# Down's last block: stores of the last results on one queue, one result turned right behind its product, and a product that goes on in another's banks

## The chip, the cores and the metric

One Trainium2 chip, one of its cores. The metric is the device time of one execution in microseconds, as a median of several runs.

## The reference

A decoder block on 512 tokens with 2048 channels, all in float32: three token mixers, an output projection, and a SwiGLU feed-forward network. Only its last line matters here:

```python
h2 = _rms_norm(x, norm2_g[l])
x = x + (jax.nn.silu(h2 @ w_gate[l]) * (h2 @ w_up[l])) @ w_down[l]
```

`w_down` is 5632 by 2048. The output is the residual plus this product.

## The kernel before, in words

Float32 matrix products are made of pieces. Every operand is split into a high part and a remainder, and each tile product is three matmuls (high by high, high by low, low by high; lines 1438 to 1440 in `Down.multiply`). The weights are split just ahead of their use by `split_up_to`: ScalarE copies the high part twice (into PSUM, line 268, and into SBUF, line 269), and VectorE subtracts it to give the low part `wl` (line 270). The weights of one piece of a product are a *unit*.

The two large products of the feed-forward network are computed by a seven-product scheme on 2 by 2 blocks. The products are numbered and run in `ORDER = (7, 1, 4, 6, 5, 2, 3)`. `Down` runs twelve blocks (`t`), which alternate between two groups of 512 columns (`g`) and go through six ranges of the inner dimension. The last block, number 11, has `end` set; blocks 10 and 11 have `final` set.

In one block each of the seven products is computed into two PSUM banks (`a` = 0 and 1). There are four such banks, used in turn, so that a product comes to stand in the banks of the one two before it. Products 7, 1, 5 and 2 start their banks afresh; 4, 6 and 3 go on in what 7, 1 and 5 left there (`fresh` in `product`). The last product of the last block (`tail`) is an exception: it starts all its banks afresh. When a product is complete, `done` puts the banks on the sums: `y[g, i, k, a]`, 128 by 512 tiles in SBUF. Sum (i, k) is channel half i and token half k. The banks go, after product 7, into sum (1,1); after 1 into (0,0); 4 into (1,0); 6 into (1,1), (0,1) and (1,0); 5 into (1,1) and, in the last block alone, into (0,1); 2 into (0,0); 3 into (0,1). Most of this is done by VectorE, which reads the bank (line 1448).

A complete sum must leave the chip with channels as rows. `turn_back` transposes it in 32 by 32 pieces on VectorE into a tile `z` (line 1355; it waits for the buffer of `z`). `put` stores one `z` with four DMAs of 128 KB, each in runs of 256 bytes (line 1365). Each DMA signals one of eight completion semaphores, which are dealt out in turn in the order of the program, whichever queue a DMA is issued on. A DMA waits on its queue until the DMA that had its semaphore before has landed.

Nothing schedules by itself: `later(n, ...)` puts a step in `evacs` or `extras`, and `run` takes the next entry of each list ahead of and behind each unit. `evacs` holds sums and turns, `extras` holds stores.

The last block ends like this. After product 6, sum (1,0) is turned and stored on SP's queue. After product 5, both `less` and both `add` run, then (1,1) is turned in two later steps, and its four stores are issued on **ACT's** queue. After product 2, ScalarE copies each of the two banks into SBUF (line 1486) and GpSimd adds the copies to sum (0,0) (line 1448 on POOL). Product 3 is the `tail` (lines 1393 to 1426). It runs in three pieces: n=0 is bank a=0 with 512 columns, n=1 bank a=1 with columns 0 to 255, n=2 bank a=1 with columns 256 to 511, which stands in the first bank of product 2. Behind the matmuls of n=0 VectorE gets the two turns of (0,0), whose `put` goes on SP, and then the sum of n=0 with (0,1) (line 1417) and half a turn; behind n=1 again a sum and half a turn, and a `put` of half size (four DMAs of 64 KB). Ahead of n=2, TensorE transposes the other half of a=0 into the bank pair `sides` (`turn(0)`, line 1403), which needs the sum of n=0. After the sum of n=2 it does the same for a=1 (`turn(1)`); VectorE and ScalarE copy `sides` into the two `end` tiles (line 1406), and two DMAs of 128 KB on SP's queue store them (line 1425). These are the last stores.

Of the kernel before, what the change touches and what calls it, by code (L numbers as in the profile page):

```python
# [17 lines left out]
T = 512  # L18
# [48 lines left out]
TH = T // 2  # L67
# [48 lines left out]
def kernel(ctx: ExitStack, tc: tile.TileContext, xT, wi, wo, wgu, wd, cst_in, outT):  # L116
    nc = tc.nc
# [19 lines left out]
    def slot(name, dt=F32, cols=T):  # L137
        return sp.tile([P, cols], dt, name=name, tag="s")

    def bank(name, cols=T, pool="banks"):  # L140
        return psum[pool].tile([P, cols], F32, name=name, tag="b")


    units = [wi[0][:, :TH], wi[0][:, TH:T], wi[0][:, T:], wi[1][:, :T], wi[1][:, T:]] + [wi[u] for u in range(2, 2 * N_IN)]
# [143 lines left out]
    def sums_now():  # L288
        for fn in sums.pop(at["use"], ()):
            fn()  # L290
# [38 lines left out]
    b = bank("idle")  # L329
    for i in range(WARM):  # L330
        nc.tensor.matmul(b, idle, idle[:, None, :].to_broadcast([P, NT, P]), start=True, stop=True)
    b = idle = None
# [101 lines left out]
    for k in range(KT):  # L434
# [21 lines left out]
        hi, lo = h_hl.pop(k)  # L456
# [22 lines left out]
    def project(name):  # L479
        b = bank(name, pool="tiles")  # L480
        for half in range(2):
            wh, wl = next_unit()
            for kk in range(8):
                k = 8 * half + kk
                s = slice(kk * P, (kk + 1) * P)
                mm3(b, wh[:, s], wl[:, s], h_hi[k], h_lo[k], k == 0, k == KT - 1)
                if kk == 3:
                    lows_now()
                if kk % 2 == 1:
                    ticks.tick()  # L490
        return b
# [445 lines left out]
    for name in PROJ[HEAD4:]:  # L937
# [4 lines left out]
        b = project(name)  # L942
# [17 lines left out]
    b = box = boxes = shared = None  # L960
# [81 lines left out]
    for half in range(2):  # L1042
        for i, n in enumerate(OUT_ORDER[half]):
            if half == 1 and i == 2:
                open_banks(banks=2, high=2)
            b = bank(f"o{half}_{n}", pool="tiles")
# [21 lines left out]
    b = m_hi = m_lo = r1b = mult_a = bias_a = bias_c = over = upper = None  # L1068
# [17 lines left out]
    evacs, extras = [], []  # L1086
# [10 lines left out]
    def run(queue):  # L1097

        for fn, *args in queue.pop(0) if queue else ():
            fn(*args)  # L1100

    def later(n, fn, *args, queue=evacs):
        while len(queue) <= n:
            queue.append([])
        queue[n].append((fn, *args))
# [59 lines left out]
    class Up:  # L1165
# [4 lines left out]
        def product(self, q):  # L1170
            banks = outs[:2]
            outs[:] = outs[2:] + banks
            for c in range(2):
                sums_now()
                run(evacs)
                wh, wl = next_unit()
                for a, b in enumerate(banks):
                    high, low = slice(a * P, (a + 1) * P), slice(TH + a * P, TH + (a + 1) * P)
                    for f in range(2):
                        x, s = ops[q, self.first + 2 * c + f], slice(f * T, (f + 1) * T)  # L1180
                        nc.tensor.matmul(b, x[:, high], wh[:, s], start=c == f == 0 and q in (7, 1, 5, 2), stop=False,  # L1181
                                         skip_group_check=True)
                        nc.tensor.matmul(b, x[:, high], wl[:, s], start=False, stop=False, skip_group_check=True)  # L1183
                        nc.tensor.matmul(b, x[:, low], wh[:, s], start=False, stop=c == f == 1, skip_group_check=True)  # L1184
                yield
                run(extras)
            later(0, self.done, self.first == 0, q, banks)
# [89 lines left out]
    y = {}  # L1277
# [70 lines left out]
    def turn_back(key, lo=0, hi=T):  # L1348

        g, i, k, a = key  # L1350
        if (g, i, k) not in pairs_out:
            name, c = BACK[g, i, k]
            pairs_out[g, i, k] = wp.tile([P, 1024], F32, name=f"z{g}{i}{k}", tag=f"raw{final_bufs[c][name]}", bufs=1)
        z = pairs_out[g, i, k].rearrange("p (b a j) -> p a b j", a=2, j=32)[:, a, lo // 32:hi // 32]
        nc.vector.transpose(z, y[key][:, lo:hi].rearrange("p (b j) -> p b j", j=32))
        if hi == T:
            y.pop(key)
# [10 lines left out]
    class Down:  # L1368
# [9 lines left out]
        def product(self, k, q):  # L1378
            banks = outs[:2]
            outs[:] = outs[2:] + banks  # L1380
            fresh = q in (7, 1, 5, 2)
            tail = self.end and k == 6
            units = []
            for c in range(2):
                sums_now()
                run(evacs)
                units.append((next_unit(), list(enumerate(self.pairs[2 * c:2 * c + 2]))))
                if not tail:
                    for a in range(2):
                        self.multiply(q, banks[a], units[c:], a, 0, T, c == 0 and fresh, c == 1)  # L1390
                    load_next(1, FEED)
                    run(extras)
            if tail:

                out = banks + outs[:1]
                sides = psum["high"].tile([P, 2, T], F32, name="sides", tag="h")
                last = [slot(f"end{c}")[:, :TH].rearrange("p (b a j) -> p b a j", a=2, j=32) for c in range(2)]

                def turn(a):

                    src = y[self.sum(0, 1, a)]
                    for c in range(2):
                        nc.tensor.transpose(sides[:, c, a * P:(a + 1) * P], src[:, TH + c * P:TH + (c + 1) * P], ident)
                    for c in range(2):
                        eng, copy = ((nc.vector, nc.vector.tensor_copy), (nc.scalar, nc.scalar.copy))[c if a else 1]
                        copy(last[c][:, :, a], sides[:, c, a * P:(a + 1) * P].rearrange("p (b j) -> p b j", j=32))

                for n, (a, lo, hi) in enumerate(((0, 0, T), (1, 0, TH), (1, TH, T))):
                    if n == 2:
                        turn(0)  # L1410
                    self.multiply(q, out[n], units, a, lo, hi, True, True)
                    if n == 0:
                        for b in range(2):
                            turn_back(self.sum(0, 0, b))
                        put(self.g, 0, 0)
                    t = y[self.sum(0, 1, a)][:, lo:hi]
                    nc.vector.tensor_add(t, t, out[n][:, lo:hi])
                    if n < 2:
                        turn_back(self.sum(0, 1, a), 0, TH)
                    if n == 1:  # L1420
                        put(self.g, 0, 1, 0, TH)
                turn(1)
                for c in range(2):
                    to = 512 * self.g + TH + c * P
                    nc.sync.dma_start(outT.rearrange("n p t -> (n p) t")[to:to + P, TH:], last[c].rearrange("p b a j -> p (b a j)"))
                return
            if self.drops:
                for j in self.pairs:
                    acts.pop((q, j))
            later(0, self.done, q, banks)  # L1430
# [35 lines left out]
        def done(self, q, banks):  # L1466
            for a, b in enumerate(banks):
                if q == 7:
                    self.add(1, 1, a, b)
                elif q == 1:  # L1470
                    self.add(0, 0, a, b)
                elif q == 4:
                    self.add(1, 0, a, b)
                elif q == 6:
                    if a:
                        later(0, self.six, a, b)
                    else:
                        self.six(a, b)
                elif q == 5:
                    self.less(1, 1, a, b)  # L1480
                    if self.end:
                        self.add(0, 1, a, b)
                elif q == 2 and self.end:

                    t = slot(f"last{a}")
                    nc.scalar.copy(t, b)
                    self.add(0, 0, a, t, nc.gpsimd)
                else:
                    self.add(0, q - 2, a, b)
            if self.end and q in (6, 5):  # L1490
                for a in range(2):
                    later(a, turn_back, self.sum(1, int(q == 5), a))
                if q == 6:
                    later(2, put, self.g, 1, 0, queue=extras)
                else:
                    later(1, put, self.g, 1, 1, 0, T, (nc.scalar,))
            if q == 3 and self.final:
                for n, (i, k) in enumerate(((0, 0), (1, 1), (1, 0), (0, 1))):
                    for a in range(2):
                        later((2, 3, 6, 7)[n] + a, turn_back, self.sum(i, k, a))  # L1500
                    later((4, 5, 8, 9)[n], put, self.g, i, k, queue=extras)
# [90 lines left out]
```

## Time and profile before

| | us |
|---|---|
| median of 3 runs (lowest, highest) | 1854.37 (1854.19, 1854.62) |
| the profiled execution | 1854.02 |
| its span, first to last instruction | 1852.0 |

The profile's times are in microseconds from the start of the span. An engine name with a q (ACTq, SPq, DVEq) is its instruction queue: a DMA issue there occupies the engine's queue while it lasts. PE is TensorE, PEld its weight load, DVE VectorE, ACT ScalarE, POOL GpSimd. In rows of the timeline the columns are start, duration, engine, line, operation, output and inputs; in brackets stands the idle time of the engine ahead of it and what ended that. Matmuls overlap, so that their distance from start to start counts, not their duration.

### The profile page before, as it was taken

To read this page: it belongs to the slowest core of one execution; us is meant where nothing else is said; L and a number is where in the kernel's file an instruction comes from. 1 tells how busy PE (TensorE), PEld (TensorE's weight loads), DVE (VectorE), ACT (ScalarE), POOL (GpSimd) and SP (SyncE) were. 2 spreads that over 40 slices of the span, in tenths; PEclk is the share of its full clock that TensorE was granted. 3 is DMA by queue.
4 is the path that set the end of the run, shared out by engine and by line. 5 is a ranking of instruction groups with operands and counts; after the bars stand their busy time and mean duration, and the time that the engine had idled before them with its cause. 6 is when DMAs were issued, how large, how long until landed. Compare 5 with 4: busy or idle time off the path is not lost.

```text
span 1852.0 us, 26517 instructions
## 1 busy us (share of the span) xinstructions
PE 1841.2 (99%) x8370; PEld 1528.2 (83%) x8370; DVE 1439.5 (78%) x2056; ACT 1318.3 (71%) x1792; POOL 1011.0 (55%) x776
## 2 busy tenths in 40 slices
PE   9999999999999999999999999999999999999997
PEld 7888888888888888888888888888888888888886
DVE  6778878998689777777777777777777777777777
ACT  6355644553458788887888888888887778877774
POOL 0135533100003557886788777877775578775652
PEclk9999999999999999999999999999999999999998
DMA  7253253344343457777867777678687579977535
GB/s 275 76 148 85 83 138 105 90 122 137 122 146 103 114 153 188 193 213 181 225 179 209 210 183 221 182 197 224 175 280 256 196 229 309 275 267 246 187 122 91
DMA packets 382987, 330.35 MB, mean 178 GB/s; under 512 B 171648, under 2 KB 311552, under 8 KB 382848
## 3 DMA queue, kind: packets, MB, share of 16 engines
q1 hardware_dynamic: 380592, 328.14, 60.9%
q8 instruction: 66, 1.08, 0.3%
q10 hardware_dynamic: 2256, 0.53, 0.2%
q14 instruction: 73, 0.60, 0.1%
HBM read 255.56 MB, written 64.63 MB: 173 GB/s over the span
## 4 chain that ended last, share of the span: by engine, by line
PE 98%; DMA 1%; DVE 0%; ACT 0%; issue 0%; POOL 0%; POOLq 0%; SPq 0%; DVEq 0%
PE out L1181 15%; PE out L1183 15%; PE out L1184 15%; PE out L1438 7%; PE out L1439 7%; PE out L1440 7%; PE o L307 3%; PE o L308 3%; PE o L309 3%; PE cq L307 2%; PE cq L308 2%; PE cq L309 2%; PE ak L307 1%; PE aq L307 1%; PE av L307 1%; PE aq L309 1%
## 5 line engine op out<-in xcount | busy, mean ns | idle before, releaser
L1181 PE MATMUL out<-wh,h 128*128 128x512 f32 x1232 | 479.4, 389 | 0.0
L1184 PE MATMUL out<-wh,h 128*128 128x512 f32 x1232 | 479.3, 389 | 0.0
L1183 PE MATMUL out<-wl,h 128*128 128x512 f32 x1232 | 479.3, 389 | 0.0
L1184 PEld LDWEIGHTS out<-wh,h 128*128 128x128 f32 x1232 | 231.3, 188 | 48.1
L1181 PEld LDWEIGHTS out<-wh,h 128*128 128x128 f32 x1232 | 231.3, 188 | 48.0
L1183 PEld LDWEIGHTS out<-wl,h 128*128 128x128 f32 x1232 | 231.3, 188 | 47.7
L1438 PE MATMUL out<-wh,a 128*128 128x512 f32 x620 | 241.2, 389 | 0.1
L1439 PE MATMUL out<-wl,a 128*128 128x512 f32 x620 | 241.0, 389 | 0.0
L1440 PE MATMUL out<-wh,a 128*128 128x512 f32 x620 | 240.9, 388 | 0.0
L274 ACT CAST wh<-w 128x1024 fp32r<-128x1024 f32 (+2 forms) x94 | 96.9, 1031 | 152.8 <-PE o L308 64.5
L1448 DVE TENSOR_TENSOR y<-y,out 128x512 f32<-128x512 f32 x192 | 128.1, 684 | 44.8 <-PE out L1440 43.4
L252 DVE TENSOR_TENSOR wl<-w,wh 128x1024 fp32r<-128x1024 f32 (+2 forms) x95 | 113.3, 1193 | 41.4 <-ACT wh L274 39.6
L1439 PEld LDWEIGHTS out<-wl,a 128*128 128x128 f32 x620 | 117.0, 189 | 24.5 <-DVE wl L270 0.4
L1438 PEld LDWEIGHTS out<-wh,a 128*128 128x128 f32 x620 | 117.0, 189 | 24.3 <-ACT wh L269 0.5
L1440 PEld LDWEIGHTS out<-wh,a 128*128 128x128 f32 x620 | 117.0, 189 | 23.8
L518 DVE SCALAR_TENSOR_TENSOR y<-bu,cst,y 128x511 f32<-128x511 f32 (+14 forms) x120 | 89.9, 749 | 0.7
L307 PE MATMUL o<-mh_c,wh 128*128 128x512 f32 x128 | 51.1, 399 | 0.0
L307 PE MATMUL cq<-hh,wh 128*128 128x512 f32 x128 | 50.5, 395 | 0.0
L309 PE MATMUL o<-mh_c,wl 128*128 128x512 f32 x128 | 50.0, 391 | 0.0
L308 PE MATMUL cq<-hl,wh 128*128 128x512 f32 x128 | 49.9, 390 | 0.0
L308 PE MATMUL o<-ml_c,wh 128*128 128x512 f32 x128 | 49.9, 390 | 0.0
L309 PE MATMUL cq<-hh,wl 128*128 128x512 f32 x128 | 49.9, 390 | 0.0
(2362 smaller groups left out, 4768.2 us busy)
## 6 DMA issues: line engine op xcount, KB each, us to landing
od<-a SPq DMA_DIRECT2D x154, 256.0 KB, 4.2
a<-od SPq DMA_DIRECT2D x154, 256.0 KB, 5.3
w<-in_wi SPq DMA_DIRECT2D x58, 512.0 KB, 3.5
w<-in_wo SPq DMA_DIRECT2D x32, 512.0 KB, 3.4
x<-in_xT SPq DMA_DIRECT2D x16, 256.0 KB, 7.0
xr<-in_xT SPq DMA_DIRECT2D x16, 256.0 KB, 3.7
x2d<-xr SPq DMA_DIRECT2D x16, 256.0 KB, 2.0
z<-x2d SPq DMA_DIRECT2D x64, 64.0 KB, 3.8
```

The lines of the kernel that those rows point to most:

```text
L252: fn(*args)
L274: (nc.vector.tensor_copy if u == 0 else nc.scalar.copy)(hi[:, :n], t[:, :n])
L307: nc.tensor.matmul(out, wh, xh, start=start, stop=False)
L308: nc.tensor.matmul(out, wh, xl, start=False, stop=False)
L309: nc.tensor.matmul(out, wl, xh, start=False, stop=stop)
L1181: nc.tensor.matmul(b, x[:, high], wh[:, s], start=c == f == 0 and q in (7, 1, 5, 2), stop=False, skip_group_check=True)
L1183: nc.tensor.matmul(b, x[:, high], wl[:, s], start=False, stop=False, skip_group_check=True)
L1184: nc.tensor.matmul(b, x[:, low], wh[:, s], start=False, stop=c == f == 1, skip_group_check=True)
L1438: nc.tensor.matmul(b[:, lo:hi], x[:, high], wh[:, s], start=start, stop=False, skip_group_check=True)
L1439: nc.tensor.matmul(b[:, lo:hi], x[:, high], wl[:, s], start=False, stop=False, skip_group_check=True)
L1440: nc.tensor.matmul(b[:, lo:hi], x[:, low], wh[:, s], start=False, stop=last, skip_group_check=True)
L1448: getattr(eng, op)(t, t, src)
```

## The change

Four things, all in the last block:

- product 3 no longer starts its two banks afresh for n=0 and n=1: it accumulates on what product 5 left in them. Product 5's result is therefore not added to (0,1) any more, save for the 256 columns that n=2 computes in another bank (a half-size add for a=1);
- after each `less` of product 5, (1,1) is turned at once, in the same step;
- the four stores of (1,1) go on SP's queue;
- product 2's result is added to (0,0) by VectorE from the banks, as in the other blocks; ScalarE's copies and GpSimd's adds are gone.

Behind line 1479 the changed kernel's lines are numbered 4 lower, and the half-size add is its line 1485.

```diff
-                    self.multiply(q, out[n], units, a, lo, hi, True, True)
+                    self.multiply(q, out[n], units, a, lo, hi, n == 2, True)
...
                 elif q == 5:
                     self.less(1, 1, a, b)
                     if self.end:
-                        self.add(0, 1, a, b)
-                elif q == 2 and self.end:
-
-                    t = slot(f"last{a}")
-                    nc.scalar.copy(t, b)
-                    self.add(0, 0, a, t, nc.gpsimd)
+                        turn_back(self.sum(1, 1, a))
+                        if a == 1:
+                            t = y[self.sum(0, 1, a)][:, TH:]
+                            nc.vector.tensor_add(t, t, b[:, TH:])
+                            later(0, put, self.g, 1, 1)
                 else:
                     self.add(0, q - 2, a, b)
-            if self.end and q in (6, 5):
+            if self.end and q == 6:
                 for a in range(2):
-                    later(a, turn_back, self.sum(1, int(q == 5), a))
-                if q == 6:
-                    later(2, put, self.g, 1, 0, queue=extras)
-                else:
-                    later(1, put, self.g, 1, 1, 0, T, (nc.scalar,))
+                    later(a, turn_back, self.sum(1, 0, a))
+                later(2, put, self.g, 1, 0, queue=extras)
```

## The prediction

> **What bounds the kernel now.** I read the page first, then the chain that ended last in its final 24 us, then who waited for whom there on the engines and on SP's queue, then the timeline.
>
> ```profile
> span 1852.0 us, 26517 instructions
> ...
> PE 98%; DMA 1%; DVE 0%; ACT 0%; issue 0%; POOL 0%; POOLq 0%; SPq 0%; DVEq 0%
> ```
>
> 98% of the chain is TensorE, and the change takes no matmul away. What it can win lies in the other 2%. Of the chain's last 24 us (start, length, what), these pieces matter:
>
> ```profile
> 1835.77 0.63 DVE z L1355
> ...
> 1838.67 0.59 ACT last L1486
> ...
> 1839.33 1.26 POOL y L1448
> 1840.59 1.23 POOLq L1587
> ...
> 1842.48 0.66 DVE y L1417
> ...
> 1843.18 0.69 PE sides L1403 x2
> ```
>
> ```profile
> ACT last L1486 <- DMA out_T<-z: 6.0, 1, 6.0
> PE sides L1403 <- DVE y L1417: 5.5, 2, 4.5
> DVE z L1355 <- POOL y L1448: 4.7, 2, 4.2
> ```
>
> Read upwards: TensorE stands 4.5 us ahead of the transposes of `turn(0)`, for the sum of n=0 on VectorE. VectorE executes in order, and ahead of that sum stand the two turns of (0,0), which wait 4.2 us for GpSimd. GpSimd waits for ScalarE's copies of product 2. ScalarE executes in order too: ahead of its copies stand the four store issues of (1,1), which wait until VectorE has turned (1,1) at 1836.4 and then occupy the queue.
>
> The second reading is SP's queue. The first row is its longest wait; the others are its issues and ACT's.
>
> ```profile
> SPq L1365 <- DMA out_T<-z: 11.9, 1, 11.9
> ```
>
> ```profile
> 1822.36 2.18 SPq L1365 DMA_DIRECT2D out_T<-z  x4
> ...
> 1826.47 0.32 SPq L1365 DMA_DIRECT2D out_T<-z  x1
> ...
> 1836.42 2.20 ACTq L1365 DMA_DIRECT2D out_T<-z  x4
> ...
> 1838.68 10.08 SPq L1365 DMA_DIRECT2D out_T<-z  x15
> ...
> 1848.86 0.88 SPq L1425 DMA_DIRECT2D out_T<-end  x2
> ```
>
> After one store at 1826.47 SP does nothing for 11.9 us. Its next store has the semaphore of ACT's first store of (1,1), which stands earlier in the program but is issued only at 1836.42. So 15 stores are pushed out in one go from 1838.68 to 1848.76, and the last two follow 0.1 us later: SP's queue and the chain through TensorE end almost together. A change to one alone would gain little; this one touches both.
>
> **The change, part by part.** The terms rest on these rows of the timeline:
>
> ```profile
> 1830.47 2.44 DVE L1448 TENSOR_TENSOR y<-y,out 128x512 f32<-128x512 f32 x4
> 1832.84 1.21 DVE L270 TENSOR_TENSOR wl<-w('11', 'd11A')_17315,wn 128x1024 fp32r<-128x1024 f32 x1
> 1833.97 0.69 DVE L1355 STREAM_TRANSPOSE z<-y 128x512 f32<-128x512 f32 x1
> 1834.59 1.19 DVE L270 TENSOR_TENSOR wl<-w('11', 'd11B')_17338,wn 128x1024 fp32r<-128x1024 f32 x1
> ```
>
> ```profile
> 1834.29 0.40 PE L1439 MATMUL out<-wl,a 128*128 128x512 f32 x1
> ...
> 1835.45 0.40 PE L1438 MATMUL out<-wh,a 128*128 128x512 f32 x1
> ...
> 1835.83 0.50 PE L1439 MATMUL out<-wl,a 128*128 128x512 f32 x1
> ...
> 1838.28 0.28 PE L1439 MATMUL out<-wl,a 128*128 128x256 f32 x1
> ...
> 1838.40 0.28 PE L1440 MATMUL out<-wh,a 128*128 128x256 f32 x1
> ...
> 1842.48 0.65 DVE L1417 TENSOR_TENSOR y<-y,out 128x512 f32<-128x512 f32 x1
> 1843.16 0.45 DVE L1355 STREAM_TRANSPOSE z<-y 128x256 f32<-128x256 f32 x1
> ...
> 1843.53 0.56 PE L1438 MATMUL out<-wh,a 128*128 128x256 f32 x1
> 1843.53 0.38 DVE L1417 TENSOR_TENSOR y<-y,out 128x256 f32<-128x256 f32 x1
> ...
> 1846.02 0.41 PE L1440 MATMUL out<-wh,a 128*128 128x256 f32 x1
> 1846.89 0.42 DVE L1417 TENSOR_TENSOR y<-y,out 128x256 f32<-128x256 f32 x1 [2.50 <-PE out L1440]
> ...
> 1848.23 0.29 DVE L1406 COPY end<-sides 128x128 f32<-128x128 f32 x1 [0.91 <-PE sides L1403]
> ```
>
> *VectorE.* It loses two full adds of product 5 and gains one of half size, gains the two adds of product 2, and gets its turns of (1,1) earlier. Distances from start to start, from these rows: an add 0.60; an add whose result is turned next 0.68 (1842.48 to 1843.16); a turn 0.62 (1833.97 to 1834.59); `wl` 1.13 (1832.84 to 1833.97) and on to its end 1.2; a half turn 0.37 (1843.16 to 1843.53). The half add lies between 0.3 (half of a full one) and 0.60; I take 0.35, its duration of 0.38 at 1843.53 less some overlap. The upper end would use up the slack found below and cost 0.12. It starts at 1830.47 as before, since nothing ahead of it changes: 1830.47 + 0.68 + 0.62 + 0.68 + 0.62 + 0.35 = 1833.42 for the first `wl`, 0.58 later than before. It ends at 1834.63. The second starts at 1834.55, as before, and ends at 1835.74. Then two adds of product 2 (1835.65, 1836.25), two turns of (0,0) (1836.85, 1837.47, the second over at 1838.18), and the sum of n=0 at 1838.09, over at 1838.74. It depends on no other engine but TensorE's n=0, below.
>
> *TensorE.* Its first matmul with the first `wl` ran at 1834.29 and now waits until 1834.63 + 0.05 = 1834.68: +0.39. Behind it stands the rest of product 3. The second `wl` held it 0.15 before (1835.45 to 1835.83 is 0.38 where 0.23 is the distance, five of them from 1834.29 to 1835.45); it is now in time. So n=0 and n=1 shift by 0.24: n=1 ends at 1838.40 + 0.28 + 0.24 = 1838.92. The sum of n=0 was over 0.13 earlier, so `turn(0)` does not wait. It starts at 1838.92 instead of 1843.18: **−4.26**. The accumulation on product 5's banks adds no matmul. Products 4, 6 and 3 do so in the other blocks. It must wait for `less` and the half add, over by 1833.5; n=0 begins at 1834.1 and n=1 at 1837.1, so both reads are covered. If they were not, each us of delay would cost one.
>
> *The clock.* Here the columns are length, then per engine busy time and count, the granted clock, the DMA share, GB/s.
>
> ```profile
> 1840.00:1841.00 1.00, 0.00 (x0) 0.00 (x0) 0.38 (x1) 0.00 (x0) 1.00 (x2) 0.86 0.97 174
> 1841.00:1842.00 1.00, 0.00 (x0) 0.00 (x0) 0.49 (x2) 0.00 (x0) 0.81 (x1) 0.50 1.07 221
> ```
>
> A mean of 0.86 over the first of these two stretches is full clock until 1840.7, 2.0 us after the last matmul's end at 1838.68, and half from there on. So n=2 ran at 0.226 us a matmul (1843.53 to 1846.02, 11 distances) where n=1 had 0.12 (1838.28 to 1838.40). Without the gap it keeps the full clock: 11 × 0.106 = 1.17, and 0.41 − 0.28 = 0.13 on the last one: **−1.30**.
>
> *The transposes.* They show at half clock alone. The two of `turn(0)` hold n=2 up by 0.35 (1843.18 to 1843.53), the two of `turn(1)` take 0.7. Bounds: unchanged, or scaled by 0.12/0.226, which is −0.16 and −0.33. I take **−0.3** for all four, nearer to the scaled end, since the other matmuls scale so. The Trainium skill, "TensorE: Matmul & The Clock Gate", section "Part 4: PE-mode transpose", says that the full clock does not engage for transposes. By that the sum would be 0.3 us smaller; no run so far shows it.
>
> *SP's queue.* It gets four issues (2.18 us by the row at 1822.36) and loses the wait of 11.9 us: in the built program all these stores are on one queue, each waiting for the one eight places before it. Issues: (0,1) of the other group, 1826.5 to 1828.7; (1,0), whose second turn stands just ahead of the add of 1830.47, from 1830.6 to 1832.8; (1,1) behind its second turn, 1833.1 to 1835.3; (0,0) behind its second turn, 1838.2 to 1840.4; the half put behind the second half turn (1839.52 + 0.45 = 1840.0) 1840.4 to 1842.6 at the worst, if its smaller stores take as long. By the terms above the sum of n=2 starts 4.26 + 1.30 + 0.15 = 5.71 earlier, at 1841.2, and VectorE's `end` copy, over at 1848.23 + 0.29 = 1848.52 before, is over at 1842.5 to 1842.8. So the queue is free just in time; the four issues cost nothing while that holds, and one for one beyond. The first of the last two issues came 0.34 behind the copy, because the queue was busy until 1848.76; it can gain that 0.3.
>
> *ScalarE and GpSimd* lose the copies, adds and issues of the chain; nothing else is left there that could be late, only the `end` copies.
>
> **Sum**: 4.26 + 1.30 + 0.3 = 5.86, and 0 to 0.3 from the last issues; I take 0.25. That is 6.1 off a span of 1852.0, hence 1845.9, and 1854.02 becomes 1847.9 for the profiled execution. The median lies 0.35 above that execution, so the forecast is **1848.3** (−0.33%). The terms' own bounds give 5.4 (transposes and issues at nothing, the half add at its upper end) to 6.4 (both in full): 1848.0 to 1849.0.
>
> **Rivals.**
>
> *Data, not issue, paces the closing.* These two windows are a `put` on its own, and the 15 stores in one go:
>
> ```profile
> 1822.36:1826.80 4.44, 4.44 (x21) 3.67 (x20) 4.44 (x7) 2.93 (x4) 0.00 (x0) 1.00 0.71 118
> ...
> 1838.68:1848.76 10.08, 3.91 (x16) 3.25 (x16) 3.90 (x8) 1.70 (x5) 2.48 (x2) 0.60 1.00 190
> ```
>
> And from issue to landing, first line 1365, then line 1425:
>
> ```profile
> DMA to landing us min/median/max: 2.1/2.8/3.4
> ...
> DMA to landing us min/median/max: 1.8/1.8/1.8
> ```
>
> A `put` of 512 KB keeps all 16 DMA engines 0.71 × 4.44 = 3.15 us busy. The last store of (0,0), issued at 1839.7, lands at 1842.5 to 1843.1; the half put is 1.6 us of data more, and `end`, 256 KB at 190 GB/s, 1.35 more: 1845.4 to 1846.0. Before, the last store landed at 1849.4 + 1.8 = 1851.2, 0.8 ahead of the span's end; so the span ends at 1846.2 to 1846.8 and the time is 1848.6 to 1849.2. For it: the engines were full in the second window. Against: the rate there was higher than 118. The Trainium skill, "DMA: Bandwidth & Descriptors", section "Issuing engines are not separate DMA queues", speaks for it and against the edit of the queue: stores issued anywhere run on the same 16 engines, and a second issuing engine saves issue time only. By that, taking four stores off ACT brings no bandwidth; the 11.9 us on SP are another thing, a wait. Chance 0.15.
>
> *VectorE becomes the bound.* Its chain from 1830.47 to 1838.74 has 0.13 us of slack, and 12 steps in a row. If each of its four turns, which wait for a sum just made, costs 0.45 more, `turn(0)` waits 1.7 and the time is 1850.0. Against: the distance of 0.68 is itself that of such a pair. Chance 0.1.
>
> *The change does not free TensorE.* If TensorE's new wait of 0.39 ahead of n=0 brings the half clock, the remaining 11 matmuls of n=0 cost 0.2 more each, n=1 and n=2 0.106 more each: 2.2 + 2.6, and 1853.1 is left, no change. Against: the clock was still full 2.0 us into the gap above. Chance 0.04.
>
> *SP's queue stalls again, worse.* Place: the stores of (1,1), now ahead of everything that follows on SP. If one of them waits for a landing, (0,0), the half put and `end` stand behind it. It decides once the landing that is waited for comes after 1842.6; the time is over 1858.1, slower than now by 0.2%, if it holds `end` back by 10 us, which takes a wait nearly as long as the one of 11.9. Against: here each waits only for a store of its own queue, and the stores land in 2.1 to 3.4 us. Chance 0.03.
>
> **How the numbers follow.** Forecast 0.68, data 0.15, VectorE 0.10, half clock 0.04, SP's stall 0.03. 0.2% is 3.7 us, about what a measurement of this kernel can tell from no change. The first three are faster by more (0.93), the half clock is within (0.04), the last is slower (0.03). The range reaches from the sum's good end less some for terms that all fall well, 1846.9, to the VectorE rival, 1850.1; that leaves out 0.07 for the last two and some 0.1 for terms beyond their bounds.
>
> **What would show it.** Right: the wait of ACT for a store is gone; no wait of SP of over 3 us for a landing; TensorE's wait ahead of `turn(0)` under 0.3; granted clock 1.00 through n=2, matmuls 0.12 apart; the first `wl` 0.5 to 0.7 later and a wait for it of 0.3 to 0.5 on PEld; last issues at 1842.6 to 1843.4. Wrong: TensorE waiting for VectorE's line 1417 for over 1 us; SP still issuing line 1365 when the `end` copies are over, by more than 0.5; the half clock ahead of 1840.

## The result, and the profile after

| | before | changed |
|---|---|---|
| median of 8 runs (lowest to highest), us | 1854.53 (1854.03 to 1856.01) | 1849.3 (1848.79 to 1850.01) |
| ratio, with its 95% interval | | 0.997 (0.996 to 0.9981) |
| span of the profiled execution, us | 1852.0 | 1847.2 |
| *closing*, us | 27.4 | 21.7 |

The change saves 5.2 us, 0.28%. Single executions differ by more than 1 us in the part that the change does not touch: in the profiles of this case the first instruction named below starts between 1824.4 and 1826.0, and once at 1827.9. So the table has a second measure, the *closing*: from the start of the `wl` (line 270) of the first unit of product 2, `w('12', 'd11A')`, to the end of the span. Up to there both kernels are the same, and yet that instruction starts 0.84 us later in the changed kernel's profile. The first row is before, the second the changed kernel:

```profile
1824.62 1.21 DVE L270 TENSOR_TENSOR wl<-w('12', 'd11A')_17453,wn 128x1024 fp32r<-128x1024 f32 x1
```

```profile
1825.46 1.21 DVE L270 TENSOR_TENSOR wl<-w('12', 'd11A')_17453,wn 128x1024 fp32r<-128x1024 f32 x1
```

So the closing is 1852.0 − 1824.62 = 27.38 before and 1847.2 − 1825.46 = 21.74 after: 5.64 us less. A time of the changed kernel is set against one of before by taking 0.84 off.

The page of the changed kernel:

```profile
span 1847.2 us, 26513 instructions
...
PE 99%; DVE 1%; DMA 0%; issue 0%; SPq 0%; ACT 0%; DVEq 0%
```

The two waits for a store's landing, 11.9 us on SP and 6.0 on ACT, are gone. These are the waits of the changed kernel's last 22 us that answer to those of before (total, times, longest):

```profile
PE sides L1403 <- DVE y L1417: 0.6, 1, 0.6
PE out L1439 <- DVE wl L270: 0.3, 1, 0.3
```

```profile
SPq L1365 <- DVE z L1355: 6.1, 3, 2.4
```

TensorE's 4.5 us ahead of `turn(0)` has gone, and the 0.6 us are those ahead of `turn(1)`. The new wait of 0.3 for `wl` is there. SP now waits only for VectorE, for its turns and 0.8 us for the half-size add, and no longer for a landing. The timeline of TensorE, VectorE and ScalarE:

```profile
1834.36 1.21 DVE L270 TENSOR_TENSOR wl<-w('11', 'd11A')_17315,wn 128x1024 fp32r<-128x1024 f32 x1
...
1835.62 0.50 PE L1439 MATMUL out<-wl,a 128*128 128x512 f32 x1 [0.33 <-DVE wl L270]
...
1839.59 0.28 PE L1440 MATMUL out<-wh,a 128*128 128x256 f32 x1
...
1839.73 0.44 PE L1403 MATMUL sides<-ident,y 128*128 128x128 f32 x2
1839.93 0.36 PE L1438 MATMUL out<-wh,a 128*128 128x256 f32 x1
...
1841.32 0.28 PE L1440 MATMUL out<-wh,a 128*128 128x256 f32 x1
1841.64 0.42 DVE L1417 TENSOR_TENSOR y<-y,out 128x256 f32<-128x256 f32 x1 [0.69 <-PE out L1440]
1842.20 0.41 PE L1403 MATMUL sides<-ident,y 128*128 128x128 f32 x2 [0.60 <-DVE y L1417]
1842.72 0.29 DVE L1406 COPY end<-sides 128x128 f32<-128x128 f32 x1 [0.66 <-PE sides L1403]
1843.04 0.27 ACT L1406 COPY end<-sides 128x128 f32<-128x128 f32 x1 [2.40 <-DVE end L1406]
```

n=2 follows n=1 with only the two transposes between them, and its 12 matmuls lie 0.12 apart, but for the first two (0.20, behind the transposes). And SP's last issues:

```profile
1839.13 0.32 SPq L1365 DMA_DIRECT2D out_T<-z  x1
...
1841.41 0.61 SPq L1365 DMA_DIRECT2D out_T<-z  x1
...
1843.36 0.47 SPq L1365 DMA_DIRECT2D out_T<-z  x1
1843.92 0.41 SPq L1425 DMA_DIRECT2D out_T<-end  x1
1844.43 0.38 SPq L1425 DMA_DIRECT2D out_T<-end  x1
```

Here is the new end. (0,0) is stored from 1839.13, the half put from 1841.41, and the queue is free at 1843.83, although VectorE's `end` copy was over at 1843.01 and ScalarE's at 1843.31. The last two stores leave 0.9 us later than they could. Before, SP's queue and the chain through TensorE ended together; now SP's queue ends alone.

### The profile page after: what moved, and what is told of

Read it like the earlier page. It is cut to its first block, busy times and chain, and to the rows that moved or that the text cites. A ratio compares the mean times of both kernels' runs of the same rounds, so it can differ in the third digit from the quotient of the medians.

```text
span 1847.2 us, 26513 instructions
## 1 busy us (share of the span) xinstructions
PE 1840.5 (100%) x8370; PEld 1527.3 (83%) x8370; DVE 1439.1 (78%) x2057; ACT 1317.3 (71%) x1790; POOL 1007.3 (55%) x774
## 4 chain that ended last, share of the span: by engine, by line
PE 99%; DVE 1%; DMA 0%; issue 0%; SPq 0%; ACT 0%; DVEq 0%
PE out L1184 15%; PE out L1183 15%; PE out L1181 15%; PE out L1439 7%; PE out L1438 7%; PE out L1440 7%; PE o L309 3%; PE o L308 3%; PE o L307 3%; PE cq L307 2%; PE cq L308 2%; PE cq L309 2%; PE ak L307 1%; PE aq L307 1%; PE av L307 1%; PE aq L309 1%
```

## The experiments

The theory, **A**: a store on ACT's queue shares completion semaphores with SP's stores, so that SP stands until it lands, and whatever comes behind it on ACT stands too. Taking the stores of (1,1) off ACT frees both chains, and after that SP's queue is the bound. The rival, **B**: the queue matters for issue time only; the gain comes from the shorter chain over VectorE, or the data of the stores set the end anyway. Times are medians; the kernel before, run beside them, has 1854.5 for experiments 1 to 4, 1854.4 for 5 to 8 and 1854.6 for 9. The three groups ran on different chips, so the ratios compare better across groups than the medians, and their intervals of about 2 us to each side are too wide for steps of 1 us. For these a place in the profile serves, the *last leave*: the start of the first of the two `end` stores, counted from the start of the closing. It is 24.2 us before (1848.86 − 1824.62) and 18.5 in the changed kernel (1843.92 − 1825.46).

**1. The queue alone.** Kernel before, with one line changed:

```diff
-                    later(1, put, self.g, 1, 1, 0, T, (nc.scalar,))
+                    later(1, put, self.g, 1, 1)
```

> Kernel before, with one edit: the four stores of (1,1) go on SP's queue instead of ACT's. The closing is measured from the start of the wl (line 270) of w('12','d11A') to the end of the span: 27.4 us before, 21.7 us in the changed kernel. Theory A (a store on ACT's queue shares completion semaphores with SP's stores, so SP stands until it lands, and ACT's own copies stand behind it): this edit alone frees both chains. ScalarE copies product 2 at once, GpSimd is through by 1836.5 of the time of before, turn(0) does not wait; SP issues (1,1) behind 1836.4 and ends about 0.2 us later than in the changed kernel. Closing 21.5 to 22.3, time about 1849.5, nearly the whole gain. Theory B (which queue it is matters only for issue time; the chain over ScalarE and GpSimd is what costs): SP gets four more issues, the chain loses ACT's 2.2 us of issues only; closing about 25, gain 2 to 2.5 us.

Measured: 1849.93 us, ratio 0.9974 (0.9964 to 0.9984); closing 23.3. That is 4.1 of the 5.6 us, against 2.4 by B and 5.1 to 5.9 by A. The mechanism is A's; its size was missed by 1 us. The chain through TensorE is as short as in the changed kernel: VectorE's `end` copy is over 17.55 us into the closing in both (1842.19 − 1824.64, 1843.01 − 1825.46). What remains is SP's queue:

```profile
1836.44 0.32 SPq L1365 DMA_DIRECT2D out_T<-z  x1
...
1838.72 0.64 SPq L1365 DMA_DIRECT2D out_T<-z  x1
...
1841.72 0.56 SPq L1365 DMA_DIRECT2D out_T<-z  x1
...
1843.42 1.25 SPq L1365 DMA_DIRECT2D out_T<-z  x1
1844.77 0.40 SPq L1425 DMA_DIRECT2D out_T<-end  x1
```

(1,1) from 1836.44, (0,0) from 1838.72, the half put from 1841.72 stand back to back. One single issue took 1.25 us, where the three ahead of it took 0.49 to 0.56. Why is not shown: the DMA engines' busy share fell to 0.34 in its last 0.47 us, so they were not full. Without these 0.8 us the closing would be 22.5, near A's upper end. The stores of (1,1) come too late because it is turned late.

**2. The adds alone.** Kernel before, without the branch of product 2 that goes over ScalarE and GpSimd:

```diff
-                elif q == 2 and self.end:
-
-                    t = slot(f"last{a}")
-                    nc.scalar.copy(t, b)
-                    self.add(0, 0, a, t, nc.gpsimd)
                 else:
                     self.add(0, q - 2, a, b)
```

> Kernel before, with one edit: product 2 is added to (0,0) by VectorE from its banks, without ScalarE's copies and GpSimd's adds; the stores of (1,1) stay on ACT's queue. Theory A: SP still stands until ACT's first store lands at 1838.7, then pushes 15 stores out by 1848.8; TensorE's wait of 4.5 us is gone, but the end is SP's. Closing 27.0 to 27.4, gain 0 to 0.4 us. Theory B: TensorE is freed and that is the gain: closing 22 to 23, gain 4.5 to 5 us.

Measured: 1854.57 us, ratio 0.9998 (0.9989 to 1.0008); closing 27.6. This is A's answer, 0.2 above its range. TensorE is freed: ScalarE's last `end` copy is over at 1843.09. But SP still stands 11.9 us, and the last stores leave 6 us after the copies (wait on SP, then issues on ACT, copy on ACT, last issues on SP):

```profile
SPq L1365 <- DMA out_T<-z: 11.9, 1, 11.9
```

```profile
1836.53 2.21 ACTq L1365 DMA_DIRECT2D out_T<-z  x4
...
1842.82 0.27 ACT L1406 COPY end<-sides 128x128 f32<-128x128 f32 x1 [2.40 <-DVE end L1406]
...
1849.20 0.90 SPq L1425 DMA_DIRECT2D out_T<-end  x2
```

A wait of 4.5 us on the engine that holds 98% of the chain was removed, and nothing was gained: another chain ended just as late.

**3. The stores back on ACT, all else changed.**

```diff
-                            later(0, put, self.g, 1, 1)
+                            later(0, put, self.g, 1, 1, 0, T, (nc.scalar,))
```

> Changed kernel, with the four stores of (1,1) put back on ACT's queue; all else as changed, so ACT has nothing behind them that hurries. Theory A: SP's first store of the other group's (0,1) has the semaphore of ACT's first store, which lands about 2.3 us after its issue behind the turn of (1,1); SP stands 8 to 9 us, and 16 stores follow in one go; closing about 23.7, 2 us longer than the changed kernel. Theory B: four issues less on SP, none of them in the closing; closing 21.7 or 0.1 less, no difference.

Measured: 1852.09 us, ratio 0.9986 (0.9977 to 0.9996); closing 25.5. B's "no difference" falls. A named the direction and the wait on SP, but the loss is 3.7 us by the closing (2.8 by the medians) where it expected 2.0:

```profile
SPq L1365 <- DMA out_T<-z: 11.0, 1, 11.0
```

```profile
ACT wn L268 <- DMA out_T<-z: 5.6, 1, 5.6
...
PE out L1438 <- ACT wh L269: 1.4, 1, 1.4
```

What A had too small is the wait. ACT's first store is issued at 1833.82, 8.7 us into the closing, and lands 2.3 us later; the 8 to 9 us leave that landing out. SP goes on at 1836.13, 11.0 into the closing, and 16 stores follow without a pause until 1847.38, just ahead of the `end` stores. The second pair of rows is a side effect: with `later(0, ...)` the stores come to stand on ACT ahead of the copies of the last weights (lines 268, 269). ScalarE waited 5.6 us behind them, and TensorE 1.4 us for the weights. This does not set the end, since the `end` copies are over at 1844.97, 2.5 us before their stores leave.

**4. Other stores on ACT.** Changed kernel, with the stores of (0,0) on ACT, which is idle there:

```diff
-                        put(self.g, 0, 0)
+                        put(self.g, 0, 0, 0, T, (nc.scalar,))
```

> Changed kernel, with the four stores of (0,0), the last full put, on ACT's queue instead of SP's; ACT is idle there. In the changed kernel SP's queue ends last: it issues (0,0) and then the half put until 0.9 us after the end copies are over. Theory B (issue time): SP is free at the half put at once, ends 2 us earlier, and the end stores go 0.8 us earlier; closing 20.9, 0.8 shorter than the changed kernel. Theory A: SP's second store of the other group's (0,1) has the semaphore of ACT's first store of (0,0) and stands until it lands, 14 us; then 15 stores in one go take 10 us. Closing about 29, 7 to 8 us longer than the changed kernel, slower than before.

Measured: 1856.39 us, ratio 1.0011 (1.0001 to 1.002); closing 29.0, as A had it. Only the queue of four stores differs from the changed kernel, and 7 us are lost:

```profile
SPq L1365 <- DMA out_T<-z: 13.7, 1, 13.7
```

```profile
1839.43 2.23 ACTq L1365 DMA_DIRECT2D out_T<-z  x4
...
1851.71 0.89 SPq L1425 DMA_DIRECT2D out_T<-end  x2
```

In all four kernels in which SP stands, it goes on 2.3 us after ACT's first issue, as that store lands: at 1838.68 before (issue at 1836.42), at 1838.79 in experiment 2 (1836.53), at 1836.13 in experiment 3 (1833.82), at 1841.69 here (1839.43).

The text ahead of the prediction says that semaphores are dealt out "in the order of the program"; that is not quite so. By the built programs, stores on ACT get theirs in between those of SP's stores of the other group's (1,0), wherever they stand in the code: it is an order in which the two queues are merged. No profile shows this order. What the profiles show fits it: in experiment 3 the first store of the next `put` on SP stands, in the other three the second.

**5. Queue and turn.** Kernel before, with the stores on SP and (1,1) turned right behind each `less`; product 2 and the banks as before:

```diff
                     if self.end:
+                        turn_back(self.sum(1, 1, a))
                         self.add(0, 1, a, b)
+                        if a == 1:
+                            later(0, put, self.g, 1, 1)
```

The later turns of (1,1) and its stores on ACT are gone, as in the change.

> Kernel before, with the stores of (1,1) on SP's queue and (1,1) turned right behind each less; product 3 still starts its banks afresh, both full adds of product 5 to (0,1) stay on VectorE, and product 2 still goes over ScalarE and GpSimd. With the queue edit alone the closing was 23.3 us, and SP's queue ended it: the stores of (1,1) still stood in front of (0,0) and the half put. Theory A (after the queue edit SP's queue is the bound, and the turn moves (1,1) out of its way): closing 21.7 to 22.1, within 0.4 of the changed kernel; the adds and the banks are worth next to nothing. Theory B (the adds on VectorE and the bank carry a share of the gain): closing 22.7 to 23.5.

Measured: 1849.2 us, ratio 0.9973 (0.9964 to 0.9983), as fast as the whole change. Its profiled execution is its slowest, 1852.4: it lost some 3 us ahead of the closing, and its last stores took 2.8 us to land instead of the usual 1.8. Its closing of 22.8 lies in B's range by the number, but 1.0 us of it is that landing. The last leave is 18.8 us into the closing (1846.68 − 1827.92), where the changed kernel has 18.5 and the queue alone 20.1:

```profile
1846.36 0.29 DVE L1406 COPY end<-sides 128x128 f32<-128x128 f32 x1 [0.66 <-PE sides L1403]
...
1846.68 0.36 SPq L1425 DMA_DIRECT2D out_T<-end  x1
```

A's first half holds: after the queue edit SP's queue was the bound, and the turn takes it off. Here the queue is free at 1845.98 and the `end` stores leave right behind VectorE's copy. The turn is worth 1.4 us in the last leave, of which 0.8 is the slow issue of experiment 1; the medians (4.6 and 5.2 us off the kernel before) can't tell. A's second half, that adds and banks are worth nothing, is only true of their sum, as the next ones show.

**6. Banks afresh.** Changed kernel, product 3 as before:

```diff
-                    self.multiply(q, out[n], units, a, lo, hi, n == 2, True)
+                    self.multiply(q, out[n], units, a, lo, hi, True, True)
...
                         turn_back(self.sum(1, 1, a))
+                        self.add(0, 1, a, b)
                         if a == 1:
-                            t = y[self.sum(0, 1, a)][:, TH:]
-                            nc.vector.tensor_add(t, t, b[:, TH:])
                             later(0, put, self.g, 1, 1)
```

> Changed kernel, with product 3 starting its banks afresh again and both full adds of product 5 to (0,1) on VectorE in place of the half one. VectorE gets 0.85 us more (two adds of 0.60 for one of 0.35) ahead of the first wl. Theory A (VectorE's chain from product 5 on sets when (0,0) is turned, and with it SP's queue): (0,0) is stored 0.85 later, closing 22.4 to 22.7. Theory B (VectorE has slack, the stores' data pace the end): closing 21.7 to 21.9.

Measured: 1849.8 us, ratio 0.9974 (0.9965 to 0.9984); closing 22.7, 1.0 more than the changed kernel, as A had it. The last leave is 19.6 us into the closing (1844.45 − 1824.90), 1.1 later. TensorE waits 1.2 us for the first `wl` instead of 0.3, and the turns of (0,0) come 0.9 later (1838.13 − 1824.90 against 1837.82 − 1825.46):

```profile
PE out L1439 <- DVE wl L270: 1.2, 1, 1.2
```

Going on in the banks is worth about 1 us in the closing, by sparing VectorE adds; the medians alone can't tell it.

**7. The half put on GpSimd's queue.** Changed kernel:

```diff
-                        put(self.g, 0, 1, 0, TH)
+                        put(self.g, 0, 1, 0, TH, (nc.gpsimd,))
```

> Changed kernel, with the four stores of the half put of (0,1) on GpSimd's queue, which has nothing else left to do and other completion semaphores than SP and ACT. Theory A (SP's issue of ten stores in a row ends the kernel): SP is free when the end copies are over, 0.9 us earlier, closing 20.8 to 21.2. Theory B (the data of the same stores pace the end, whatever queue they are on): the end stores are issued 0.9 earlier but land as late as before; closing 21.5 to 21.9. A third way: GpSimd's own issue is slow, and its stores land last; then closing is over 21.9.

Measured: 1849.43 us, ratio 0.9974 (0.9963 to 0.9984); closing 22.2. That is the third way's range, but not its reason, as the rows show. The `end` stores leave 17.6 us into the closing, 0.9 earlier as hoped, but the second issue takes 1.35 us, and they take 3.0 us to land instead of 1.8:

```profile
1841.98 0.36 SPq L1425 DMA_DIRECT2D out_T<-end  x1
1842.43 1.35 SPq L1425 DMA_DIRECT2D out_T<-end  x1
```

GpSimd needs 2.52 us to issue its four stores, once the half turn is there:

```profile
1840.19 2.52 POOL L1365 DMA_DIRECT2D out_T<-z  x4 [21.15 <-DVE z L1355]
```

That is hardly more than SP's 2.42 in the changed kernel (1841.41 to 1843.83). And GpSimd's stores do not land last: the fourth, issued at 1842.1, lands 3.1 us later at 1845.2, the second `end` store at 1845.5. What makes the `end` stores slow here stays open. Issues as slow as this one also came without GpSimd (1.25 us in experiment 1, 1.24 in experiment 9).

**8. No half put.** Changed kernel, without the line that stores it (256 channels of the second token half stay unwritten; the bracket in the expectation should read: four stores of 64 KB).

> Changed kernel, without the four stores of the half put of (0,1): 256 channels of the second token half are not stored (64 runs of 128 KB less 256 KB in all). This bounds what SP's queue and the data cost in the closing: the end stores should be issued right behind their copies. Theory A and B alike: closing 20.8 to 20.9, that is 0.9 less than the changed kernel; if it stays above 21.4, neither SP's queue nor the data were the bound.

Measured: 1848.45 us, ratio 0.9968 (0.9957 to 0.998); closing 20.8. So 0.9 us is what the half put costs in the closing. The `end` stores land 1.7 to 1.8 us after their issue, as in the changed kernel, so there they are not held up by the half put's data once they are issued.

**9. Product 2 over ScalarE and GpSimd again.** If VectorE's order decides when (0,0) can be stored, the adds on VectorE are a loss. Changed kernel, with the branch of product 2 put back:

```diff
                             later(0, put, self.g, 1, 1)
+                elif q == 2 and self.end:
+                    t = slot(f"last{a}")
+                    nc.scalar.copy(t, b)
+                    self.add(0, 0, a, t, nc.gpsimd)
                 else:
```

> Changed kernel, with one part undone: product 2 goes over ScalarE's copies and GpSimd's adds again; queue, turn and banks stay as changed. VectorE is spared two adds (1.2 us) between its last wl and the turns of (0,0). Theory A (VectorE's order decides when (0,0) is stored, and with it when SP's queue is through): with the times of the kernel with the queue edit alone, GpSimd's second add is over 11.6 us into the closing, as VectorE comes to the second turn; (0,0) is stored 1.2 us earlier than in the changed kernel, SP is free when the end copies are over; closing 20.8 to 21.3, 0.5 to 0.9 less than the changed kernel, faster than both kernels. Theory B (the adds on VectorE are a gain, or the landing of the last stores paces the end whatever is ahead): closing 21.6 or more.

> The changed kernel itself, on the same chip and in the same rounds as the one with product 2 on GpSimd: closing 21.6 to 21.9, 1849.3 us.

Measured in the same rounds: this kernel 1848.32 us (1847.47 to 1848.74), ratio 0.9966 (0.9954 to 0.9979), closing 20.7; the changed kernel 1849.31 (1847.96 to 1850.22), ratio 0.9971 (0.996 to 0.9982), closing 22.5, over what was expected by one of the last issues, which took 1.24 us instead of 0.41; its last leave is 18.5, as before. A holds, and this version is the fastest of all, by 1.0 us in the medians; the two intervals of the ratios overlap, so the last leave carries that verdict, at 17.5 us (1842.64 − 1825.10) against 18.5 in both profiles of the changed kernel. Its rows:

```profile
1836.26 1.29 DVE L1355 STREAM_TRANSPOSE z<-y 128x512 f32<-128x512 f32 x2
...
1837.58 0.32 SPq L1365 DMA_DIRECT2D out_T<-z  x1
...
1840.45 0.32 SPq L1365 DMA_DIRECT2D out_T<-z  x1
...
1842.64 0.42 SPq L1425 DMA_DIRECT2D out_T<-end  x1
1843.16 0.38 SPq L1425 DMA_DIRECT2D out_T<-end  x1
```

VectorE turns (0,0) right behind its last `wl`, 11.2 us into the closing (1836.26 − 1825.10), where the changed kernel has 12.4. (0,0) leaves 1.2 us earlier, the half put no longer waits for it, and the `end` stores leave as their copies are over.

## Why the prediction came out as it did

The forecast was 1848.3, 6.1 off; measured is 1849.3, 5.2 off by medians and 5.6 by the closing. The direction and the range of 1846.9 to 1850.1 held, and so did the mechanism but for its last term, SP's queue. The time lies outside 1848.0 to 1849.0, the bounds that the terms themselves gave. One of the prediction's own signs of being wrong came too: SP issued line 1365 until 0.52 us after ScalarE's `end` copy (0.82 after VectorE's), where over 0.5 was named. Point by point, with times of the changed kernel less 0.84 where they are set against a forecast:

- **What bounds the kernel: right, and shown.** That two chains end together, and that a change to one alone gains little, is experiment 2, which cleared TensorE's wait and gained nothing. Experiment 1 gained 4.6 us with one edit because that edit frees both: ACT's stores held SP's queue and ScalarE's copies. That SP's wait hangs on ACT's store is shown by 1, 3 and 4, since moving four stores between the two queues brings it or takes it away.
- **VectorE's chain: right.** First `wl` at 1833.52 (forecast 1833.42), sum of n=0 at 1838.19 (1838.09). Its 0.13 us of slack were just enough.
- **TensorE: right.** `turn(0)` at 1838.89 (forecast 1838.92), the wait for `wl` 0.33 on the matmul. On PEld it was 0.8, where 0.3 to 0.5 was expected.
- **The clock: right.** 0.12 us a matmul through n=2, as the granted clock of 1.00 has it. From the start of n=2's first matmul to the end of its last it was 2.90 us before (1843.53 to 1846.43) and is 1.67 now (1839.93 to 1841.60): 1.23 less, where 1.30 was forecast.

```profile
1840.00:1841.00 1.00, 1.00 (x11) 1.00 (x10) 0.91 (x3) 0.43 (x2) 0.00 (x0) 1.00 0.99 152
1841.00:1842.00 1.00, 0.60 (x6) 0.39 (x4) 0.36 (x1) 0.00 (x0) 0.00 (x0) 1.00 0.93 153
```

- **The transposes: right in sign, near the scaled bound.** Those of `turn(0)` hold n=2 up by 0.20 instead of 0.35, those of `turn(1)` take 0.41 instead of 0.66. The Trainium skill, "TensorE: Matmul & The Clock Gate", section "Part 4: PE-mode transpose", had it that the full clock does not engage for them. Here they are faster while the granted clock is 1.00, so the measurement decides against it for transposes between matmuls; whether transposes alone would bring the clock up, no run here shows.
- **From n=2 to its sum: missed, but worth nothing.** Between the end of the last matmul, as the profile models it, and VectorE's add lay 0.46 us before (1846.43 to 1846.89); now it is 0.04 (1841.60 to 1841.64). The forecast had left it as it was. It is not the clock: experiments 1 and 5 have 0.45 and 0.46 at a granted clock of 1.00. Why it went is open. The `end` copy is over at 1842.17 instead of 1842.5 to 1842.8, but SP's queue was not free, so this gained nothing.
- **SP's queue: the step that failed.** "So the queue is free just in time; the four issues cost nothing while that holds". The queue was free at 1842.99, not 1842.6: the half put began at 1840.57 instead of 1840.4 and its four issues took 2.42 us instead of 2.2. The sum had the first of the last two stores at 1842.75 (the copy over at 1848.52 − 5.86 = 1842.66, and 0.09 behind it); it left at 1843.08, 0.33 later. From there to the end of the span it took 3.28 us instead of 3.14. Together these are the 0.5 by which 6.1 became 5.6; the rest to 5.2 is within what two executions differ by. Had the `end` copy come when the forecast had it, the queue would have been late by 0.3 instead of 0.8.
- **ScalarE and GpSimd.** "nothing else is left there that could be late" is true. But the two adds that VectorE takes over were counted in its chain as if they cost nothing, since TensorE does not wait for them. Experiment 9 shows the price: they hold the turns of (0,0) back by 1.2 us, and with them SP's queue by 0.9 and the closing by 1.0.
- **The rivals.** VectorE as the bound, half clock from the short wait, a stall on SP: none came. Experiment 4 shows a stall: 13.7 us of wait cost 7.1 us, less than the 10 that the rival named. Data pacing the closing is not settled, and by the number it did better than the forecast: it had 1848.6 to 1849.2. The DMA engines are 0.9 and more busy from 1840 to 1844 of the changed kernel's profile and 0.8 in the us after, so issue and data end close together. Against it: the `end` stores land after 1.8 us with and without the half put ahead of them (experiment 8). What may still hold is that full DMA engines slow the issues themselves; experiments 7 and 9 do not tell.

Taken apart along one path, with the gain over the kernel before in the medians of the same rounds:

| | gain, us | last leave, us | closing, us |
|---|---|---|---|
| before | | 24.2 | 27.4 |
| queue (experiment 1) | 4.6 | 20.1 | 23.3 |
| and the turn (5) | 5.2 | 18.8 | 22.8 |
| and the banks (9) | 6.3 | 17.5 | 20.7 |
| and the adds on VectorE: the change (9) | 5.3 | 18.5 | 22.5 |

Only the first step is clear of noise in the medians; for the others the last leave speaks, one profile each and two for the change.

## What to carry to other kernels

When a store waits for a landing, ask whose semaphore it waits for: a store issued late on another queue can hold a whole queue that has nothing to do with it. At the end of a kernel follow every chain that ends there, the queues among them; freeing one engine is worth what the next chain leaves. And a part of a change that shortens a chain can lengthen another: try each part without the others, since here three parts were better than four.

## What the runs showed of the hardware

- The issue of the first store of 128 KB on a queue that stood idle takes 0.32 us, of the next three 0.49, 0.52 and 0.73 (from 1822.36 before, and again from 1839.13 in the changed kernel). These are equal stores, so a queue's time can't be had from their count alone. Single issues took 1.24 to 1.35 us (experiments 1, 7 and 9); in 1 and 9 the DMA engines' busy share fell to 0.34 and 0.26 meanwhile, so full engines are not the reason there.
- The clock fell to half 2.0 us after the last matmul in the kernel before. In the changed kernel the last matmul ended at 1841.6 and the transposes at 1842.6, and the clock was full until 1846.5. By the mean granted clock of each us, the time from the last matmul to half clock was 2.0 to 5.3 us in the twelve profiles: it is not fixed. It was nowhere under 2.0, which fits that TensorE's new wait of 0.33 cost no clock.
- The last stores took 1.8 us to land in most profiles, 2.8 in experiment 5, 3.0 in 7, and 1.8 and 2.6 in the changed kernel's second one.
- Four stores of 64 KB issued by GpSimd occupied it for 2.5 us, and their landing took 3.1 to 4.3. The same four on SP occupied it for 2.4 us and landed after 1.9 to 2.6 in the changed kernel.
